# A two-block transformer kernel: modulation rows through GpSimd's queue, projection weights split after the squares' additions, a third gate tile ahead of the first latent product

## Chip, cores and metric

One core of one Trainium2 chip runs the whole program. The metric is device time in microseconds; of three timed executions the median counts.

## What is computed

256 tokens with 1024 channels pass through three layers: a retention layer, a latent-attention layer, each followed by a gated projection of a side input `p`, and a third layer with convolution, pooling and a feed-forward part, whose normalisations are modulated by a vector computed from `c_2`. Cut to what the change touches:

```python
# layers 0 and 1
h = rms_norm(x, pre_norm_g[i])
y = retention_branch(h, ...)  or  mla_branch(h, ...)     # both end in  (silu(gate) * o) @ w_out
x = x + rms_norm(y, post_norm_g[i])
x = x + (p[i] @ ple_w_proj[i]) * sigmoid(x @ ple_w_gate[i])
# inside mla_branch
c_q = rms_norm(z[..., :o1], q_norm_g); c_kv = rms_norm(z[..., o1:o2], kv_norm_g)
q = c_q @ w_uq                                           # the first latent product
# layer 2
mod = silu(c) @ w_ada + b_ada                            # 1024 x 6144, split in six vectors
h = layer_norm(x) * (1 + sc1) + sh1                      # and so on with g1, sh2, sc2, g2
```

All tensors are float32.

## The kernel before

Activations lie transposed, channels on partitions. Every large product is made exact enough by splitting: a weight tile `raw` of 128 x 1024 comes by DMA (512 KB), ScalarE rounds it to `wh` (L176, `A.copy`), VectorE subtracts to get the rest `wl` (L177, `V.tensor_sub`), and TensorE adds three products (`mm`, L232 to L234). One such load of eight 128 x 128 tiles feeds 24 matmuls. There are six buffers for `raw`, five each for `wh` and `wl`. `Seq` hands out the tiles of a list of entries in order and calls `load` whenever a new 1024-wide tile begins.

The program is written as one long stream. `tick` counts a nominal TensorE time, and `after(us, fn)` places side work (norm statistics, softmax steps) at a later point of that stream. But the order in which an engine gets its instructions is made by a planner at build time: whatever is ready in its plan and has a free buffer may go ahead of work that was written earlier and is not ready. Among ready instructions the earlier written one goes first. `tc.keep_in_program_order(i)` pins an instruction behind the last one that was written before it for the same engine. On the chip each engine then takes its instructions strictly in the planned order and waits at the head of its queue.

Three places matter.

- **Modulation rows.** `ada_steps` (L398 to L416) goes through 48 rows of 128 x 1024 of `w_ada`. `fetch` brings one row (512 KB) into one of two buffers `adach` (tag `ada1`); L408 multiplies it on VectorE with silu(c) and sums into a column of `mod`. The fetch of row n+2 stands behind the reduction of row n, goes through SP's queue and is pinned there, so it is issued at the point of the stream at which `ada()` is called. SP's queue also carries all weight fetches (L163). `mod_rate` sets how often `ada()` is called: every 10 us in the retention layer, every 1.8 us in the first part of `ret_out`, every 7.61 and 12.84 us in the latent layer. The last eight rows are called from `late_steps` near the end. They make `g2`, which goes to DRAM and back as a broadcast row (`g<-mod`, `half<-g`, L1366 and L1370) for the last normalisation.
- **Projection weights.** `out_proj` runs the layer's output product in two parts: the first twelve of sixteen blocks of channels for all eight outputs m, then the last four. In the second part `done` feeds finished pairs to `Sums`: ScalarE squares them (L322), VectorE adds the squares (L326, "the squares' additions"), and after m = 7 TensorE sums over channels with a matrix of ones (L336). The statistics (L374, L376, L362 to L368) follow, then `post` scales (L679), adds the residual (L680) and splits. `prepared()`, called in `post`, fetches and splits the two weight tiles of `p @ ple_w_proj` and multiplies them; that product fills TensorE while the statistics are made. These two loads are written behind all loads of the output product.
- **Gate tiles.** In the latent layer `mla_gate(g)` makes two of 16 gate blocks (two loads, 48 matmuls) and needs only the normalised input. `mla_proj(p)` is the first to need the latent vectors, which come out of `lora` (L772 to L780, split at L185 and L186). Two gate tiles are made ahead of `mla_proj(0)`, two more ahead of `mla_proj(1)`.

GpSimd's queue carries little: some memsets, the two fetches of `p` (L712), and at the end the broadcast rows and one addition.

Of the kernel before, what the change touches and what calls it, by code (L numbers as in the profile page):

```python
# [11 lines left out]
F32 = mybir.dt.float32  # L12
# [7 lines left out]
P = 128  # L20
# [62 lines left out]
def tile_kernel(ctx, tc, order, xT, pT, pos, vec, cst, cv, rows, wada, wts, outT):  # L83
    nc = tc.nc
    V, A, T = nc.vector, nc.scalar, nc.tensor
# [11 lines left out]
    def nm(s):  # L97
        uid[0] += 1
        return f"{s}_{uid[0]}"
# [4 lines left out]
    def bank2():  # L104
        return bank().rearrange("p (b t) -> p b t", b=2)

    class Blk:

        def __init__(self, nb, dt=F32):
            self.t = [hp_.tile([P, 4, S], dt, tag="half", name=nm("half")) for _ in range((nb + 3) // 4)]  # L110
# [21 lines left out]
    def t2(dt=F32):  # L132
        return tp.tile([P, 2, S], dt, tag="t2", name=nm("t2"), bufs=6)
# [6 lines left out]


    class Seq:
        def __init__(self, entries, width=P, parts=True, ready=()):
            self.e, self.w, self.i, self.parts, self.ready = entries, width, 0, parts, list(ready)

        def next(self):
            per = D // self.w
            s = self.i % per
            if s == 0:
                self.h, self.l = load(self.e[self.i:self.i + per], self.w, self.parts, self.ready.pop(0) if self.ready else None)  # L150
            self.i += 1
            sl = slice(s * self.w, (s + 1) * self.w)
            return self.h[:, sl], self.l[:, sl]

    def fetch(entries, width, parts=True, step=D, pinned=False):
        g = len(order)
        order.append((width, list(entries)))
        n = len(entries) * width
        tag, bufs = (("raw", 6), ("wh", 5), ("wl", 5))[0 if parts else [0, 1][g % len([0, 1])]]
        raw = wp.tile([P, D], F32, tag=tag, name=nm("raw"), bufs=bufs)  # L160
        for o in range(0, n, step):
            e = min(n, o + step)
            d = nc.sync.dma_start(out=raw[:, o:e], in_=wts[g, :, o:e])  # L163
            if pinned:
                tc.keep_in_program_order(d)
        return raw[:, :n]

    def load(entries, width, parts=True, raw=None):
        if raw is None:
            raw = fetch(entries, width, parts)  # L170
        if not parts:
            return raw, raw
        n = raw.shape[1]
        hi = wp.tile([P, D], F32R, tag="wh", name=nm("wh"), bufs=5)[:, :n]
        lo = wp.tile([P, D], F32R, tag="wl", name=nm("wl"), bufs=5)[:, :n]
        A.copy(hi, raw)  # L176
        V.tensor_sub(lo, raw, hi.bitcast(F32))  # L177
        return hi, lo

    def nouter(name, ms, kbs, c0=0):  # L180
        return [(name, kb * P, c0 + m * P) for m in ms for kb in kbs]

    def split(hi, lo, src, scale=None):
        if scale is None:
            A.copy(hi, src)  # L185
            V.tensor_sub(lo, src, hi.bitcast(F32))  # L186
        else:
            A.activation(hi, src, AF.Copy, scale=scale)
            V.scalar_tensor_tensor(lo, src, scale, hi.bitcast(F32), MUL, SUB)
# [11 lines left out]
    def after(us, fn):  # L201
        queue.append((clk[0] + us, fn))
        queue.sort(key=lambda e: e[0])
# [4 lines left out]
    def mod_rate(us):  # L208
        mods["rate"], mods["last"] = us, clk[0]
# [13 lines left out]
    def drain():  # L223
        busy[0] = True
        while queue:
            due, fn = queue.pop(0)
            clk[0] = max(clk[0], due)
            fn()
        busy[0] = False

    def mm(ps, l, r, first, last):
        T.matmul(ps, l[0], r[0], start=first, stop=False)  # L232
        T.matmul(ps, l[0], r[1], start=False, stop=False)  # L233
        T.matmul(ps, l[1], r[0], start=False, stop=last)  # L234
        tick(3 * r[0].shape[-1] / 2400.0)
# [5 lines left out]
    def rhs(pair, kb):  # L241
        return pair[0][kb], pair[1][kb]
# [35 lines left out]
    def col(name, i, n=1):  # L278
        o = VOFF[name] + i
        return vc[:, o:o + n]  # L280
# [117 lines left out]
    def ada_steps():  # L398
        def fetch(n):
            ch = sp.tile([P, D], F32, tag="ada1", name=nm("adach"), bufs=2)  # L400
            tc.keep_in_program_order(nc.sync.dma_start(out=ch, in_=wada[n * P:(n + 1) * P, :]))
            return ch

        have = [fetch(0), fetch(1)]
        yield
        for n in range(48):
            ch = have.pop(0)
            V.tensor_tensor_reduce(ch, ch, sc, 1.0, 0.0, MUL, ADD, mod[:, n:n + 1])  # L408
            if n + 2 < 48:
                have.append(fetch(n + 2))  # L410
            if n % 8 == 7:
                m = slice(n - 7, n + 1)
                V.tensor_add(mod[:, m], mod[:, m], col("b_ada_2", n - 7, 8))
            yield
# [11 lines left out]
    def ada():  # L426
        mods["n"] += 1
        next(ada_it, None)
# [181 lines left out]
    def out_proj(name, pairs, ka, rate, done, layer):  # L610
        ys = proj_banks()
        mod_rate(rate)
        seq = Seq(nouter(name, range(8), range(ka)) + nouter(name, range(8), range(ka, 16)))
        for m in range(8):
            for kb in range(ka):
                mm(ys.at(m), seq.next(), rhs(pairs, kb), ys.starts(m) and kb == 0, False)
        drain()
        mod_rate(None)
        prep = ple_proj(layer)
        for m in range(8):  # L620
            for kb in range(ka, 16):
                mm(ys.at(m), seq.next(), rhs(pairs, kb), False, kb == 15 and ys.ends(m))
            if ys.ends(m):
                done(m, ys)
        return ys, prep

    class proj_banks:
# [81 lines left out]
    def ple_proj(layer):  # L709
        php = [tp.tile([P, 2, S], F32R, tag="fa", name=nm("php"), bufs=3) for _ in range(2)]  # L710
        raw = t2()
        nc.gpsimd.dma_start(out=raw, in_=pT[:, 2 * layer:2 * layer + 2, :])  # L712
        split(php[0], php[1], raw)

        def prepared():
            seq = Seq(nouter(f"ple_proj{layer}", range(8), range(2)))
            tiles = [seq.next() for _ in range(16)]
            prj = Blk(DB)
            for i in range(4):
                ps = bank2()  # L720
                for b in range(2):
                    for kb in range(2):
                        mm(ps[:, b, :], tiles[(2 * i + b) * 2 + kb], (php[0][:, kb, :], php[1][:, kb, :]), kb == 0, kb == 1)
                A.copy(prj.pair(i), ps)
            return prj
        return prepared

    sums, done = proj_sums(False, lambda m, ys: ys.piece(m), "r")
    ys, prep = out_proj("ret_out", ret_g, 12, 1.8, done, 0)
    xt = post(xt, ys, sums, 0, prep)  # L730

# [54 lines left out]
    seq = Seq([e for kb in range(8) for e in (("mla_kr", kb * P, 0), ("mla_in", kb * P, 768), ("mla_in", kb * P, 896))])  # L786
# [9 lines left out]
    seq = Seq(nouter("mla_in", range(6), range(8)))  # L796
# [13 lines left out]
    def mla_gate(p):  # L810

        if p % 2 == 0:
            sgs[p // 2] = Blk(4)
        ps = bank2()
        for b in range(2):
            for kb in range(8):
                mm(ps[:, b, :], seq_g.next(), rhs(xp, kb), kb == 0, kb == 7)
        gr = t2()
        V.scalar_tensor_tensor(gr, ps, -0.5, bc2(r1["nr"]), MUL, MUL)
        A.activation(sgs[p // 2].pair(p % 2), gr, AF.Silu)  # L820
# [97 lines left out]
    mod_rate(7.61)  # L918
    ng = 0
    for p in range(8):  # L920
        while ng < [2, 4, 6, 8, 8, 8, 8, 8][p]:
            mla_gate(ng)
            ng += 1
        if p == 4:
            mod_rate(12.84)
        mla_proj(p)
        after(3.07, lambda p=p: mla_scores(p))

    sums, done = proj_sums(False, lambda m, ys: ys.piece(m), "m")
    ys, prep = out_proj("mla_out", mla_g, 12, 2.27, done, 1)  # L930
    xt = post(xt, ys, sums, 1, prep)

# [144 lines left out]
    def conv():  # L1077
        next(conv_it, None)
# [251 lines left out]
    seq = Seq([e for i in range(NA + 2, FB) for e in nouter("w_up", [i, FB + i], range(8))])  # L1330
# [6 lines left out]

    late = late_steps()
    after(1.12, lambda: every(2.6, 3 * NA + 8, lambda: next(late)))


# [3 lines left out]
    seq = Seq([("w_down", kb * P, 512 * n) for kb in kbs for n in range(2)], 512)  # L1345
# [137 lines left out]
```

## Time and profile before

| | |
|---|---|
| median of three executions | 851.39 us (851.32 to 853.29) |
| the profiled execution | 853.2 us, of which the span is 851.4 us |
| TensorE busy | 834.8 us, 98% |
| VectorE busy | 713.2 us, 84% |
| ScalarE busy | 550.6 us, 65% |
| GpSimd busy | 9.7 us, 1% |
| DMA | 167.5 MB, mean 197 GB/s; SP's queue holds 55.0% of the 16 engines' span, GpSimd's 0.9% |

Almost all of the span is TensorE's own work, so the table says little about where a change of order can matter. That is read from the waits of TensorE, and from what stands on the other engines just ahead of them.

### The profile page before, as it was taken

How to read it: one execution, taken by the hardware profiler on the slowest of the kernel's cores; microseconds unless marked ns; L12 is line 12 of the kernel's file. 1: busy time of each engine (PE TensorE's matmuls, PEld its weight loads, DVE VectorE, ACT ScalarE, POOL GpSimd, SP SyncE). 2: the span in 40 equal slices, each digit the busy share in tenths (PEclk: the TensorE clock that was granted, in tenths of full speed). 3: DMA queues.
4: the chain of work that ended last, by engine and by line, in shares of the span. 5: the costliest groups of instructions: out<-in, count | busy, mean ns of one | idle time of the engine just before them, and what ended most of it. 6: DMA issues, size and time to landing. Idle time of an engine off the chain costs nothing.

```text
span 851.4 us, 15952 instructions
## 1 busy us (share of the span) xinstructions
PE 834.8 (98%) x6218; PEld 798.2 (94%) x6218; DVE 713.2 (84%) x1287; ACT 550.6 (65%) x928; POOL 9.7 (1%) x28
## 2 busy tenths in 40 slices
PE   8999999999999999999999999999999999999995
PEld 6989899999999999999999998999999999999885
DVE  6999787898889978699874677899687888889996
ACT  6656555545676686787653757999756576666550
POOL 0000000000000000000000000000000000000001
PEclk9999999999999999999999999999999999999998
DMA  9866566678557647365355354245463365567722
GB/s 334 321 233 235 204 211 245 243 254 293 188 173 243 242 150 237 136 243 179 118 168 174 142 205 156 85 174 177 146 226 134 136 194 179 194 205 253 275 86 74
DMA packets 46634, 167.48 MB, mean 197 GB/s; under 512 B 5216, under 2 KB 5472, under 8 KB 46560
## 3 DMA queue, kind: packets, MB, share of 16 engines
q1 hardware_dynamic: 45936, 164.38, 55.0%
q0 software_dynamic: 624, 2.10, 0.9%
q8 instruction: 48, 0.79, 0.4%
q14 instruction: 26, 0.21, 0.1%
HBM read 165.41 MB, written 1.05 MB: 196 GB/s over the span
## 4 chain that ended last, share of the span: by engine, by line
PE 93%; DVE 4%; DMA 1%; ACT 1%; issue 1%; DVEq 0%; SPq 0%; ACTq 0%
PE ps L233 27%; PE ps L232 26%; PE ps L234 26%; PE ps L238 10%; PE ps L336 1%; PE ps L358 1%; DVE wl L177 1%; PE ps L898 1%; DMA adach<-in_wada 1%; DMA raw<-in_wts 1%; DVE half L679 0%; ACT wh L176 0%; DVE half L680 0%; PE ps L1146 0%; DVE t L1410 0%
## 5 line engine op out<-in xcount | busy, mean ns | idle before, releaser
L232 PE MATMUL ps<-half,wh 128*128 128x256 f32 x1504 | 424.8, 283 | 1.4 <-ACT half L185 1.4
L233 PE MATMUL ps<-half,wh 128*128 128x256 f32 x1504 | 423.6, 282 | 0.6 <-DVE half L186 0.5
L234 PE MATMUL ps<-half,wl 128*128 128x256 f32 x1504 | 422.1, 281 | 0.3 <-DVE wl L177 0.3
L176 ACT CAST wh<-raw 128x1024 fp32r<-128x1024 f32 x233 | 242.9, 1048 | 147.7 <-PE ps L233 94.3
L177 DVE TENSOR_TENSOR wl<-raw,wh 128x1024 fp32r<-128x1024 f32 x233 | 282.3, 1219 | 58.3 <-ACT wh L176 55.8
L233 PEld LDWEIGHTS ps<-half,wh 128*128 128x128 f32 x1504 | 283.3, 188 | 1.9 <-DVE half L186 0.9
L232 PEld LDWEIGHTS ps<-half,wh 128*128 128x128 f32 x1504 | 282.4, 188 | 2.6 <-ACT half L185 2.0
L234 PEld LDWEIGHTS ps<-half,wl 128*128 128x128 f32 x1504 | 283.9, 189 | 0.6 <-DVE wl L177 0.5
L238 PE MATMUL ps<-half,raw 128*128 128x256 f32 (+2 forms) x384 | 84.9, 380 | 0.0
L238 PEld LDWEIGHTS ps<-half,raw 128*128 128x128 f32 x384 | 72.5, 190 | 10.0
L232 PE MATMUL ps<-wh,half 128*128 128x512 f32 (+1 forms) x202 | 72.7, 361 | 0.0
L234 PE MATMUL ps<-wh,half 128*128 128x512 f32 (+1 forms) x202 | 71.0, 351 | 0.0
L233 PE MATMUL ps<-wl,half 128*128 128x512 f32 (+1 forms) x202 | 71.0, 351 | 0.0
L408 DVE CUSTOM_DVE_ANT_0 adach<-adach,siluc 128x1024 f32<-128x1024 f32 x48 | 58.3, 1218 | 11.5 <-DMA adach<-in_wada 11.5
L1063 ACT ACTIVATE t<-apad,vec 128x256 f32<-128x256 f32 x106 | 44.3, 500 | 0.5 <-DVE half L1064 0.5
L233 PEld LDWEIGHTS ps<-wl,half 128*128 128x128 f32 x202 | 38.1, 189 | 5.5 <-DVE wl L177 0.4
L232 PEld LDWEIGHTS ps<-wh,half 128*128 128x128 f32 x202 | 38.0, 188 | 5.5 <-ACT wh L176 0.2
L234 PEld LDWEIGHTS ps<-wh,half 128*128 128x128 f32 x202 | 38.0, 188 | 5.5
L1064 DVE TENSOR_TENSOR half<-half,t 128x512 f32<-128x512 f32 x53 | 36.4, 687 | 3.7 <-ACT t L1063 1.8
L185 ACT CAST half<-t 128x256 fp32r<-128x256 f32 (+1 forms) x47 | 20.3, 452 | 16.9 <-DVE t L1323 10.9
L186 DVE TENSOR_TENSOR half<-t,half 128x256 fp32r<-128x256 f32 (+1 forms) x47 | 21.7, 483 | 3.6 <-ACT half L185 2.7
L1318 ACT ACTIVATE t<-ps,vec 128x256 f32<-128x256 f32 x38 | 21.0, 558 | 2.0 <-PE ps L234 1.2
(277 smaller groups left out, 971.1 us busy)
## 6 DMA issues: line engine op xcount, KB each, us to landing
raw<-in_wts SPq DMA_DIRECT2D x257, 512.0 KB, 4.3
adach<-in_wada SPq DMA_DIRECT2D x48, 512.0 KB, 5.1
half<-in_xT SPq DMA_DIRECT2D x4, 256.0 KB, 6.9
half<-in_rows POOLq DMA_DIRECT2D x2, 512.0 KB, 5.2
out<-t SPq DMA_DIRECT2D x4, 256.0 KB, 2.0
cst<-in_cst SPq DMA_DIRECT2D x1, 928.0 KB, 10.1
raw<-in_wts SPq DMA_DIRECT2D x2, 256.0 KB, 5.1
siluc<-in_cv SPq DMA_DIRECT2D x1, 512.0 KB, 8.1
```

Of the source, the lines that this page charges most:

```text
L176: A.copy(hi, raw)
L177: V.tensor_sub(lo, raw, hi.bitcast(F32))
L185: A.copy(hi, src)
L186: V.tensor_sub(lo, src, hi.bitcast(F32))
L232: T.matmul(ps, l[0], r[0], start=first, stop=False)
L233: T.matmul(ps, l[0], r[1], start=False, stop=False)
L234: T.matmul(ps, l[1], r[0], start=False, stop=last)
L238: T.matmul(ps, w, r, start=first, stop=last)
L408: V.tensor_tensor_reduce(ch, ch, sc, 1.0, 0.0, MUL, ADD, mod[:, n:n + 1])
L1063: A.activation(t[:, b, :], apad[:, i0 + b, k:k + S], AF.Copy, scale=w[b])
L1064: V.tensor_add(acc.pair(i0 // 2), acc.pair(i0 // 2), t)
L1318: A.activation(t[:, b, :], ps[:, b, :], AF.Identity, bias=col("b_dw_f_2", m), scale=w[2])
```

## The change

The rows of `w_ada` are fetched through GpSimd's queue and no longer pinned. The two projection loads are written after m = 5 of the second part, ahead of the last load of the output product, and their subtractions are pinned behind what VectorE was last given, the second of the squares' additions. The first latent product stands behind three gate tiles; the second then stands behind one.

```diff
     class Seq:
-        def __init__(self, entries, width=P, parts=True, ready=()):
-            self.e, self.w, self.i, self.parts, self.ready = entries, width, 0, parts, list(ready)
+        def __init__(self, entries, width=P, parts=True, ready=(), pinned=False):
+            self.e, self.w, self.i, self.parts, self.ready, self.pinned = entries, width, 0, parts, list(ready), pinned
...
     def load(entries, width, parts=True, raw=None, pinned=False):
...
         A.copy(hi, raw)
-        V.tensor_sub(lo, raw, hi.bitcast(F32))
+        sub = V.tensor_sub(lo, raw, hi.bitcast(F32))
+        if pinned:
+            tc.keep_in_program_order(sub)
         return hi, lo
...
     def ada_steps():
         def fetch(n):
             ch = sp.tile([P, D], F32, tag="ada1", name=nm("adach"), bufs=2)
-            tc.keep_in_program_order(nc.sync.dma_start(out=ch, in_=wada[n * P:(n + 1) * P, :]))
+            nc.gpsimd.dma_start(out=ch, in_=wada[n * P:(n + 1) * P, :])
             return ch
...
             if ys.ends(m):
                 done(m, ys)
+            if m == 5:
+                prep.load()
         return ys, prep
...
+        tiles = []
+
+        def load():
+            seq = Seq(nouter(f"ple_proj{layer}", range(8), range(2)), pinned=True)
+            tiles.extend(seq.next() for _ in range(16))
+
         def prepared():
-            seq = Seq(nouter(f"ple_proj{layer}", range(8), range(2)))
-            tiles = [seq.next() for _ in range(16)]
             prj = Blk(DB)
...
+        prepared.load = load
         return prepared
...
     for p in range(8):
-        while ng < [2, 4, 6, 8, 8, 8, 8, 8][p]:
+        while ng < [3, 4, 6, 8, 8, 8, 8, 8][p]:
             mla_gate(ng)
```

## Rows read from the trace of the kernel before

**Rows 1.** The page: engines' busy time, share of the span, instructions.
```profile
PE 834.8 (98%) x6218; PEld 798.2 (94%) x6218; DVE 713.2 (84%) x1287; ACT 550.6 (65%) x928; POOL 9.7 (1%) x28
```

**Rows 2.** Waits of TensorE: line, releaser, us in total, times, longest.
```profile
PE ps L336 <- DVE t L326: 2.5, 1, 2.5
PE ps L232 <- ACT half L185: 1.4, 1, 1.4
...
PE ps L898 <- DVE sm L887: 0.7, 1, 0.7
```

**Rows 3.** Timeline of TensorE, 211 to 215.5 us: start, us, instruction, idle before.
```profile
211.05 0.28 PE L234 MATMUL ps<-half,wl 128*128 128x256 f32 x1
213.83 1.53 PE L336 MATMUL ps<-t,ones 128*128 128x256 f32 x6 [2.50 <-DVE t L326]
```

**Rows 4.** Timeline of VectorE, 204 to 219 us.
```profile
205.57 1.23 DVE L408 CUSTOM_DVE_ANT_0 adach<-adach,siluc 128x1024 f32<-128x1024 f32 x1 [1.59 <-DMA adach<-in_wada]
...
206.72 4.63 DVE L177 TENSOR_TENSOR wl<-raw,wh 128x1024 fp32r<-128x1024 f32 x4
...
213.00 0.68 DVE L326 TENSOR_TENSOR t<-t,t 128x512 f32<-128x512 f32 x1
...
216.06 0.42 DVE L374 TENSOR_SCALAR t<-ps 128x256 f32<-128x256 f32 x1 [1.25 <-PE ps L336]
```

**Rows 5.** Timeline of TensorE, 282 to 286 us.
```profile
282.86 0.28 PE L233 MATMUL ps<-half,wh 128*128 128x256 f32 x1
282.98 0.28 PE L234 MATMUL ps<-half,wl 128*128 128x256 f32 x1
284.62 0.62 PE L232 MATMUL ps<-half,wh 128*128 128x256 f32 x3 [1.37 <-ACT half L185]
```

**Rows 6.** Timeline of VectorE, 278 to 293 us.
```profile
284.80 1.42 DVE L186 TENSOR_TENSOR half<-t,half 128x256 fp32r<-128x256 f32 x4
...
288.65 0.75 DVE L186 TENSOR_TENSOR half<-t,half 128x256 fp32r<-128x256 f32 x2
```

**Rows 7.** The tile adach: its instructions, who waited, time to landing.
```profile
L401 SPq DMA_DIRECT2D adach<-in_wada x48: 327/425/1447, 12.6 to 797.0; - x48
...
DMA to landing us min/median/max: 3.5/5.1/9.0
```

**Rows 8.** The tile adach by stretch: us, VectorE's share of it, clock, DMA.
```profile
163.00:200.00 37.00, 13.23 (x12) 1.00 0.81 275
200.00:222.00 22.00, 2.58 (x3) 1.00 0.74 275
```

**Rows 9.** All engines by stretch: busy us of each, clock, DMA share, GB/s.
```profile
12.00:16.00 4.00, 3.99 (x17) 2.85 (x16) 4.00 (x9) 4.00 (x8) 0.00 (x0) 1.00 1.02 409
...
163.00:166.00 3.00, 3.00 (x28) 3.00 (x27) 3.00 (x7) 1.38 (x2) 0.00 (x0) 1.00 0.88 266
```

**Rows 10.** Chain that ended last, 0 to 24 us: start, us, what.
```profile
1.65 4.71 DMA raw<-in_wts
...
6.49 5.70 PE ps L238 x8
```

**Rows 11.** Timeline of GpSimd, 0 to 200 us.
```profile
1.50 0.52 POOL L755 MEMSET kr<- 64x512 f32 x1
```

**Rows 12.** DMA issues of 160 to 161 us, and of 434 to 435 us.
```profile
t<-in_pT POOLq DMA_DIRECT2D x1, 256.0 KB, 5.4
...
t<-in_pT POOLq DMA_DIRECT2D x1, 256.0 KB, 3.5
```

**Rows 13.** Timeline of VectorE, 326 to 337 us.
```profile
328.57 1.23 DVE L408 CUSTOM_DVE_ANT_0 adach<-adach,siluc 128x1024 f32<-128x1024 f32 x1 [2.06 <-DMA adach<-in_wada]
...
335.71 0.55 DVE L887 TENSOR_SCALAR sm<-sm,sm 128x128 f32<-128x128 f32 x2
```

**Rows 14.** Timeline of VectorE, 827 to 845 us.
```profile
834.11 0.69 DVE L1387 TENSOR_TENSOR t<-ps,half 128x512 f32<-128x512 f32 x1 [4.75 <-DMA half<-g]
...
841.54 1.38 DVE L1407 TENSOR_TENSOR t<-t,half 128x512 f32<-128x512 f32 x2
```

More of the change, by code (lines that the diff above doesn't have):

```diff
@@ L149, in next @@
             if s == 0:
-                self.h, self.l = load(self.e[self.i:self.i + per], self.w, self.parts, self.ready.pop(0) if self.ready else None)
+                self.h, self.l = load(self.e[self.i:self.i + per], self.w, self.parts, self.ready.pop(0) if self.ready else None, self.pinned)
             self.i += 1
@@ L166, in fetch, with load @@
         return raw[:, :n]
-    def load(entries, width, parts=True, raw=None):
+    def load(entries, width, parts=True, raw=None, pinned=False):
         if raw is None:
```

## The prediction

> **What bounds the kernel now.** I began with the page: TensorE is busy 834.8 us, 98% of the span [rows 1]. No change of order can shorten that work, so the change is worth what it takes from TensorE's waits or adds to them. The second view is therefore the list of TensorE's waits [rows 2]. Past the start and the end of the program only three are over half a microsecond: 2.5 us for the squares' addition at L326, 1.4 us for a split of a latent vector at L185, 0.7 us for a softmax step at L887. Together that is 4.6 us, 0.54% of 851.39. A measurement of this kernel can tell about 0.3%, 2.55 us, from no change: faster means below 848.84, slower above 853.94.
>
> The third view is the timelines at these places. TensorE ends the second part of `ret_out` at 211.3 and starts the sums at 213.83, 2.50 us idle [rows 3]. VectorE shows why: at 205.57 a reduction L408 starts after waiting 1.59 us for its row, then four subtractions L177 run until 211.35, and the second addition L326 comes only at 213.00 [rows 4]. By the order of the fetches, the second and third of these four are the projection's two tiles. At the second place TensorE ends gate tile 1 at 283.3 and finds the first latent vector at 284.62 [rows 5]; the last latent split ends at 289.4 [rows 6].
>
> **The change, part by part.** The sum goes against the profiled execution's span, 851.4; it took 853.2, 1.8 us around the span. The median of the runs shown, 851.39, is 1.8 us under that execution; I carry the differences over to the median.
>
> *Third gate tile.* It moves 48 matmuls between 283.3 and the first latent product. Matmuls start 0.12 us apart there (282.86 to 282.98 [rows 5]), so the tile takes 5.8 us and TensorE arrives at 289.1, when four of the six latent vectors are long split [rows 6]; the last two need 0.3 us more and are used last. The 1.37 us [rows 5] go: **-1.4**, between -1.5 and 0. The tile's two loads come out of the same list earlier and hold two of five weight buffers while the latent vectors are made, which cover them. What is late next is the stretch up to `mla_proj(1)`, which loses 5.8 us of gates ahead of its softmax; its own gate tile and 7.6 us of planned distance cover that.
>
> *Projection subtractions.* Two subtractions of 1.16 us (4.63 over four [rows 4]) leave the stretch ahead of L326: 2.3 us of the 2.50 [rows 3]. They then stand behind the second addition. Queued behind them on VectorE are the statistics, L374; those wait for the sums anyway, and VectorE had 1.25 us idle there [rows 4], so about half of the 2.3 us comes back as delay of L374 if gate subtractions stand there too. I take **-1.3**, between -2.5 and 0. The two weight fetches pass the last output load in SP's queue and hold two `raw` and two `wh`/`wl` buffers longer; all that follows in that queue are gate weights, needed after the projection's own products. In the latent layer the wait does not show, and I cost the same edit there at nothing: VectorE has the matmuls of m = 6 and 7 to hide it, else it costs 2.3 us at most.
>
> *Rows through GpSimd.* Forty-eight issues of 0.425 us [rows 7] leave SP's queue, and no TensorE wait names a weight fetch past the start, so this alone gives nothing. What decides is the lost pin. The planner takes whatever is ready: GpSimd clears `kr` at 1.50 us [rows 11], though `kr` belongs to the latent layer. Two row buffers are free from the start, so I expect the first two fetches at about 1.5 us instead of 12.6 [rows 7]. There the transfers are the bound: TensorE's first product waits for a weight tile that takes 4.71 us to land [rows 10]. Two rows are 1.05 MB; at 409 GB/s [rows 9] that is 2.6 us of all DMA engines ahead of what TensorE waits for. If the two queues together move only 266 GB/s, as in the stretch in which GpSimd's fetch of `p` ran beside SP's [rows 9], it is 3.9 us; if the fetches are held or slip into gaps, 0. TensorE runs without a break behind that wait [rows 10], so a delay is never made up. I take **+2.5**, the nearest full-rate row.
>
> The Trainium skill speaks to this in "DMA: Bandwidth & Descriptors", section "Issuing engines are not separate DMA queues": transfers from any issuing engine run on the same 16 DMA engines and interleave, and a second issuer saves only issue time. The 266 GB/s agree with it in that the second queue brought no rate. By this rule no transfer of the change gets faster, and the start keeps its price.
>
> From then on a row is fetched as soon as its buffer is free, and reductions fill every idle moment of VectorE in the plan. By now 12 of them stand in 163 to 200 and 3 in 200 to 222 [rows 8], none in the statistics. Each takes 1.15 us (205.57 to 206.72 [rows 4]). With data always ready one may stand in the idle 1.25 us ahead of L374 [rows 4]; one that starts near the end of that moment delays the statistics by nearly its 1.15. I take **+0.8**, between 0 and 3.5 (three of them in full). In the softmax stretch the row that VectorE waited 2.06 us for [rows 13], just ahead of L887, would have landed long before: **-0.7** [rows 2], between -0.7 and +0.7. At the end, `g2` is ready early and the 4.75 us wait for its broadcast goes [rows 14]; VectorE then does the first half's products, 1.38 us at L1407 [rows 14], ahead of the last chunks. TensorE's own last products hold most of that back, so **-0.4**, between -0.5 and 0. The memsets and the fetch of `p` on GpSimd now queue behind row fetches that wait for VectorE, a few us; `p` has over 30 us until its product.
>
> Sum: 2.5 + 0.8 - 0.7 - 0.4 - 1.3 - 1.4 = -0.5. **Forecast 850.9 us**, no change that can be told.
>
> **Rivals.** *The start is not hit.* If the first two fetches do not float to the front, or their packets fit between SP's, the 2.5 us go: -0.5 - 2.5 = -3.0, **848.4**, faster. For it: the late landing of `silu(c)`, which the first reductions also need, gives a fetch at 1.5 us no use, and a planner may order by need. Against: it filled GpSimd at 1.50 with a memset far ahead of its use [rows 11].
>
> *Reductions in the way of the statistics.* The place is VectorE from 206 to 222. If three reductions stand there and the projection's gain is lost to them, it is 2.5 + 3.45 - 0.7 - 0.4 - 1.4 = +3.5, **854.9**, slower; with two it is +2.3 and not told from no change, so it decides from the third. For it: today the rows are limited by landing there (1.59 us of wait [rows 4]), the buffers are refilled at once, and nothing ends the row work at 206 any more. Also for it: GpSimd's fetch of 256 KB landed after 5.4 us where VectorE was busy throughout, after 3.5 us elsewhere [rows 12]. Against: higher-standing work goes first when both are ready.
>
> The Trainium skill, "SBUF — State Buffer", section "Who interferes with whom", would have a transfer issued from GpSimd starve while VectorE works in a two-port mode, since GpSimd cannot write the descriptors then. By it rows land later and the backlog reaches further into the statistics, this rival's time. The two landings lean that way, with one sample each.
>
> *The change does not do what it says:* the planner already had the projection's subtractions or the row fetches about where they now are, and only the gate tile counts, 851.39 - 1.4 = **850.0**.
>
> **How the numbers follow.** Forecast 0.49, start not hit 0.30, reductions in the way 0.17, only the gate tile 0.04. So faster 0.30, same 0.49 + 0.04 = 0.53, slower 0.17. The range reaches from 847.2 (the start not hit and 1.2 us more of the projection's gain) to 854.8 (just under the slow rival's middle); about 0.06 lie below and 0.12 above. The forecast's own range is 848.9 to 853.4.
>
> **What would show it.** In the trace of the changed kernel: the time of GpSimd's first two `adach` issues, and whether TensorE's first L238 starts near 6.5 or near 9 us. The wait of L336 for L326 and the count of L408 between 206 and 222. The wait of L232 for L185 near 284 gone. The wait of L1387 for `half<-g` gone. The forecast is wrong if L238 starts on time, or if any wait of TensorE over 2 us appears that rows 2 do not have.

## The result and the profile after

The changed kernel takes **899.66 us** (median of 4 runs, 897.33 to 903.42) against 852.34 us for the kernel before on the same chip (851.32 to 854.68): ratio **1.0547**, 95% interval 1.052 to 1.0574. The forecast was 850.9 us in a range of 847.2 to 854.8; the slowest rival had 854.9, so none of the cases came near. The profiled execution has a span of 895.6 us, 44.2 us over the span of before. Line numbers are slightly higher now: row fetch L403, reduction L410, squares' addition L328, ones-sums L338, group sums L360, products L234 to L236, splits L187 and L188; L176 and L177 kept theirs.

The page of the changed kernel: TensorE's busy time, the granted clock in 40 slices, and the issues of the rows.

```profile
PE 845.6 (94%) x6218; PEld 807.9 (90%) x6218; DVE 715.7 (80%) x1287; ACT 547.6 (61%) x927; POOL 35.3 (4%) x76
...
PEclk9999999999689999999999989999999999999999
...
adach<-in_wada POOLq DMA_DIRECT2D x48, 512.0 KB, 4.9
```

Against [rows 1] the work of VectorE is the same (713.2 and 715.7 us); TensorE has idle time that it hadn't, and three slices with a lower clock. The list of TensorE's waits names the places (line, releaser, us in total, times, longest):

```profile
PE ps L338 <- DVE t L328: 17.2, 2, 15.3
PE ps L234 <- ACT half L187: 9.5, 2, 5.2
PE ps L234 <- ACT t L187: 5.2, 3, 2.7
PE ps L360 <- DVE t L299: 4.1, 1, 4.1
PE ps L240 <- DMA raw<-in_wts: 3.4, 1, 3.4
```

In [rows 2] the first of these was 2.5 us in all, and the splits of the heads and the group sums did not appear. To see where the time went I take the start of the n-th matmul in both timelines and subtract. At matmul 60 (20.1 us before: the start), 1440 (202.0: the four heads are done), 1620 (227.3: past the sums and the projection of the first output), 2640 (351.9: latent attention), 3900 (502.0: past the sums of the second output) and 6180 (837.6: the end), TensorE is late by the following, in us. Each row comes from one profiled execution, and the runs in it are described in the experiments below.

| kernel | 60 | 1440 | 1620 | 2640 | 3900 | 6180 |
|---|---|---|---|---|---|---|
| changed kernel | 1.7 | 17.7 | 39.8 | 36.5 | 44.4 | 44.3 |
| gate tile alone | 1.2 | 1.1 | 0.8 | -2.0 | -1.9 | -1.9 |
| rows alone | 2.9 | 18.3 | 26.3 | 24.0 | 24.0 | 24.0 |
| projection alone | -0.5 | -0.6 | 7.0 | 8.3 | 18.2 | 18.2 |
| rows in SP's queue, no pin | -0.1 | 7.7 | 12.8 | 11.4 | 11.4 | 11.4 |
| rows, first two pinned | -0.2 | 13.8 | 21.8 | 19.6 | 19.5 | 19.5 |
| rows, reductions in place | 2.8 | 4.0 | 12.0 | 10.7 | 21.6 | 21.6 |
| projection behind the last load | -0.5 | -0.6 | -0.3 | -0.1 | 1.5 | 1.4 |

Differences of about 1 us between two traces say little: at matmul 60 the kernels whose start is unchanged already differ by -0.5 to 1.2. So 16 us went in the heads, where the prediction had no term at all, 22 us around the first sums, 8 us around the second; some 3 us came back between them.

**The first sums.** VectorE's timeline of the changed kernel (start, us, instruction, idle before):

```profile
224.91 1.22 DVE L410 CUSTOM_DVE_ANT_0 adach<-adach,siluc 128x1024 f32<-128x1024 f32 x1 [1.51 <-DMA adach<-in_wada]
...
229.36 1.22 DVE L410 CUSTOM_DVE_ANT_0 adach<-adach,siluc 128x1024 f32<-128x1024 f32 x1 [3.22 <-DMA adach<-in_wada]
...
234.62 1.23 DVE L410 CUSTOM_DVE_ANT_0 adach<-adach,siluc 128x1024 f32<-128x1024 f32 x1 [4.03 <-DMA adach<-in_wada]
...
235.77 0.69 DVE L328 TENSOR_TENSOR t<-t,t 128x512 f32<-128x512 f32 x1
239.99 1.23 DVE L410 CUSTOM_DVE_ANT_0 adach<-adach,siluc 128x1024 f32<-128x1024 f32 x1 [3.53 <-DMA adach<-in_wada]
...
241.14 0.69 DVE L328 TENSOR_TENSOR t<-t,t 128x512 f32<-128x512 f32 x1
241.74 4.62 DVE L177 TENSOR_TENSOR wl<-raw,wh 128x1024 fp32r<-128x1024 f32 x4
```

From 222 to 241 VectorE does next to nothing but wait for one row after the other: it is idle for 12.3 us (1.51 + 3.22 + 4.03 + 3.53) ahead of four reductions, and the two additions that TensorE needs stand behind the third and the fourth. ScalarE is not what they wait for: it had ended the last of their squares at 227.62. The next row is fetched only when a reduction has freed its buffer; in [rows 4] the one reduction near this place had waited 1.59 us. Then come four subtractions: the pinned two of the projection first, the last output load's third. So the products of m = 6 and 7, which had stopped at 226.6 after two matmuls each, had to wait as well. TensorE's timeline around the wait, where [rows 3] had 2.50 (the third product of each block, L236, is missing ahead of it):

```profile
226.11 0.28 PE L235 MATMUL ps<-half,wh 128*128 128x256 f32 x1
226.23 0.28 PE L234 MATMUL ps<-half,wh 128*128 128x256 f32 x1
226.35 0.28 PE L235 MATMUL ps<-half,wh 128*128 128x256 f32 x1
241.97 0.77 PE L338 MATMUL ps<-t,ones 128*128 128x256 f32 x1 [15.35 <-DVE t L328]
```

**The second sums** show the projection's part by itself, for no reduction is near (VectorE, 498 to 518 us):

```profile
498.96 1.23 DVE L177 TENSOR_TENSOR wl<-raw,wh 128x1024 fp32r<-128x1024 f32 x1 [1.64 <-ACT wh L176]
510.79 0.69 DVE L328 TENSOR_TENSOR t<-t,t 128x512 f32<-128x512 f32 x1 [10.60 <-ACT t L324]
513.62 0.69 DVE L328 TENSOR_TENSOR t<-t,t 128x512 f32<-128x512 f32 x1 [2.13 <-ACT t L324]
514.23 4.62 DVE L177 TENSOR_TENSOR wl<-raw,wh 128x1024 fp32r<-128x1024 f32 x4
```

VectorE is idle for 10.60 us and does not use it for the last output load's subtraction: that one is the third of the four at 514.23.

**The heads.** One of several like places (VectorE, 97 to 108 us); L297 and L299 feed the group sums L360, which waited 4.1 us:

```profile
103.76 1.23 DVE L410 CUSTOM_DVE_ANT_0 adach<-adach,siluc 128x1024 f32<-128x1024 f32 x1 [4.46 <-DMA adach<-in_wada]
...
104.91 0.69 DVE L297 TENSOR_TENSOR t<-t,t 128x512 f32<-128x512 f32 x1
...
105.91 0.41 DVE L299 TENSOR_TENSOR t<-t 128x256 f32<-128x256 f32 x1
```

The tile `adach` in the changed kernel: how long VectorE sat idle ahead of its reductions (us, times), and the time from issue to landing.

```profile
  DMA adach<-in_wada: 32.4, 20
...
DMA to landing us min/median/max: 3.6/4.9/8.3
```

Before, this idle time was 11.5 us in 11 waits, and the landing was as long [rows 7].

### The profile page after: what moved, and what is told of

It is laid out like the page before. It is cut to its first block, busy times and chain, and to the rows that moved or that the text cites. A ratio compares the mean times of both kernels' runs of the same rounds, so it can differ in the third digit from the quotient of the medians.

```text
span 895.6 us, 15985 instructions
## 1 busy us (share of the span) xinstructions
PE 845.6 (94%) x6218; PEld 807.9 (90%) x6218; DVE 715.7 (80%) x1287; ACT 547.6 (61%) x927; POOL 35.3 (4%) x76
## 4 chain that ended last, share of the span: by engine, by line
PE 69%; issue 17%; DVE 6%; DMA 4%; POOL 2%; ACT 2%; SPq 0%; DVEq 0%; POOLq 0%; ACTq 0%
PE ps L234 19%; PE ps L235 19%; PE ps L236 19%; PE ps L240 9%; DMA adach<-in_wada 3%; POOL adach L403 2%; DVE wl L177 2%; PE ps L338 1%; DMA half<-in_xT 1%; DVE adach L410 1%; ACT wh L176 1%; PE ps L908 1%; PE ps L360 1%; DVE half L191 0%; PE ps L1156 0%
## 5 line engine op out<-in xcount | busy, mean ns | idle before, releaser
L234 PE MATMUL ps<-half,wh 128*128 128x256 f32 x1504 | 428.1, 286 | 9.5 <-ACT half L187 9.5
L236 PE MATMUL ps<-half,wl 128*128 128x256 f32 x1504 | 424.3, 282 | 0.0
L177 DVE TENSOR_TENSOR wl<-raw,wh 128x1024 fp32r<-128x1024 f32 x233 | 282.4, 1220 | 60.1 <-ACT wh L176 57.6
L176 ACT CAST wh<-raw 128x1024 fp32r<-128x1024 f32 x233 | 241.8, 1048 | 126.0 <-PE ps L235 88.1
L234 PEld LDWEIGHTS ps<-half,wh 128*128 128x128 f32 x1504 | 285.9, 191 | 10.8 <-ACT half L187 10.3
L235 PEld LDWEIGHTS ps<-half,wh 128*128 128x128 f32 x1504 | 286.4, 190 | 1.1 <-DVE half L191 0.3
L236 PEld LDWEIGHTS ps<-half,wl 128*128 128x128 f32 x1504 | 286.5, 191 | 0.0
L410 DVE CUSTOM_DVE_ANT_0 adach<-adach,siluc 128x1024 f32<-128x1024 f32 x48 | 58.4, 1221 | 32.5 <-DMA adach<-in_wada 32.4
L234 PE MATMUL ps<-wh,half 128*128 128x512 f32 (+1 forms) x202 | 72.9, 362 | 0.0
L236 PE MATMUL ps<-wh,half 128*128 128x512 f32 (+1 forms) x202 | 71.2, 352 | 0.0
L1073 ACT ACTIVATE t<-apad,vec 128x256 f32<-128x256 f32 x106 | 44.2, 497 | 0.5 <-DVE half L1074 0.5
L236 PEld LDWEIGHTS ps<-wh,half 128*128 128x128 f32 x202 | 38.1, 189 | 5.6
L234 PEld LDWEIGHTS ps<-wh,half 128*128 128x128 f32 x202 | 38.0, 188 | 5.5 <-ACT wh L176 0.4
L403 POOL DMA_DIRECT2D adach<-in_wada x48 | 25.7, 535 | 222.7 <-DVE mod L410 214.0
L187 ACT CAST half<-t 128x256 fp32r<-128x256 f32 (+1 forms) x47 | 20.4, 452 | 16.8 <-DVE t L1333 12.1
L187 ACT CAST half<-half 128x512 fp32r<-128x512 f32 (+1 forms) x24 | 11.9, 512 | 26.1 <-DVE half L600 13.6
```

Source lines behind the costliest of these rows:

```text
L177: sub = V.tensor_sub(lo, raw, hi.bitcast(F32))
L403: nc.gpsimd.dma_start(out=ch, in_=wada[n * P:(n + 1) * P, :])
L1073: A.activation(t[:, b, :], apad[:, i0 + b, k:k + S], AF.Copy, scale=w[b])
```

## The experiments

My theory at this point: rows and projection each cost by themselves. The rows cost since VectorE works through its instructions in an order fixed beforehand, and without the pin the reductions stand where their row was supposed to have landed, with needed work behind them. The projection costs since the last output load's subtraction is handed out behind the pinned ones. The rivals: GpSimd's queue itself (slower or later transfers), and one of the two parts being harmless without the other.

**The gate tile alone.**

```diff
-        while ng < [2, 4, 6, 8, 8, 8, 8, 8][p]:
+        while ng < [3, 4, 6, 8, 8, 8, 8, 8][p]:
```

> Third gate tile alone. My theory: it is the one part that gains; the trace of the changed kernel has no idle at the first latent vector and is 1.7 to 3.4 us less late from there to the softmax stretch, so 849 to 851 us, ratio 0.996 to 0.999, and no other wait of TensorE over 1 us that the kernel before has not. Rival (the tile only moves the wait to the softmax of the next latent stretch): 851 to 852, with a wait of 1 us or more near 330.

Measured 851.31 us (10 runs), ratio 0.996, interval 0.9943 to 0.9976. TensorE's wait of 1.4 us for L185 is gone; it gains 2.8 us between matmul 1620 and 2640 (0.8 to -2.0), of which 2.0 are waits of TensorE that went (2.4 to 0.4 us in that stretch); where the rest comes from is not traced. One wait over 1 us is new (1.6 us for `wh`, L176); it lies in the first 20 us, which the edit doesn't touch. This version is faster than both kernels, by 0.4% against the one before.

**The rows alone**, through GpSimd without a pin:

```diff
-            tc.keep_in_program_order(nc.sync.dma_start(out=ch, in_=wada[n * P:(n + 1) * P, :]))
+            nc.gpsimd.dma_start(out=ch, in_=wada[n * P:(n + 1) * P, :])
```

> Rows through GpSimd's queue without a pin, nothing else. My theory: this is the larger cause. Reductions stand in VectorE's order where the row is supposed to have landed, and the critical work behind them waits; up to the third head TensorE loses what it lost in the changed kernel there, 1.7 at the start and about 2, 6, 6 and 2 us near 47, 106, 131 and 174, together 17 to 18; then the reductions of rows 38 to 43 stand among the squares' additions and cost some 10 to 16 more: 868 to 886 us. Rival (the pinned projection subtractions are what makes the 15 us wait of the sums, and reductions only fill the gap that they leave): 868 to 871, the sums' wait under 3 us.

Measured 877.47 us, ratio 1.0266 (1.0227 to 1.0304). TensorE's longest waits and VectorE's timeline, 224 to 239 us, of this run:

```profile
PE ps L336 <- DVE t L326: 8.5, 1, 8.5
PE ps L358 <- DVE t L297: 4.9, 2, 4.1
```

```profile
227.91 1.23 DVE L408 CUSTOM_DVE_ANT_0 adach<-adach,siluc 128x1024 f32<-128x1024 f32 x1 [2.20 <-DMA adach<-in_wada]
...
229.06 2.36 DVE L177 TENSOR_TENSOR wl<-raw,wh 128x1024 fp32r<-128x1024 f32 x2
233.28 1.23 DVE L408 CUSTOM_DVE_ANT_0 adach<-adach,siluc 128x1024 f32<-128x1024 f32 x1 [1.85 <-DMA adach<-in_wada]
...
235.56 0.69 DVE L326 TENSOR_TENSOR t<-t,t 128x512 f32<-128x512 f32 x1
...
237.30 0.69 DVE L326 TENSOR_TENSOR t<-t,t 128x512 f32<-128x512 f32 x1
238.57 1.23 DVE L408 CUSTOM_DVE_ANT_0 adach<-adach,siluc 128x1024 f32<-128x1024 f32 x1 [0.58 <-DMA adach<-in_wada]
```

The loss of the heads is all here (18.3 us late at matmul 1440), and so is a wait of 8.5 us for the additions: the rival, under 3 us, falls. The softmax wait at L898 of [rows 2] is gone, and so, without the gate tile, is the wait for the latent vector's split at L185: 26.3 to 24.0. The gate tile has nothing left to gain beside the rows.

**Pin or queue.** The rows left in SP's queue and only the pin taken away:

```diff
-            tc.keep_in_program_order(nc.sync.dma_start(out=ch, in_=wada[n * P:(n + 1) * P, :]))
+            nc.sync.dma_start(out=ch, in_=wada[n * P:(n + 1) * P, :])
```

> Rows left in SP's queue, only the pin of their fetch taken away. If the lost pin is the cause of what the rows cost (ratio 1.027 with GpSimd), the reductions drift here as well and the time is 865 to 885 us, ratio 1.015 or more, with reductions between the squares' additions of the first output projection. If GpSimd's queue is the cause, the time is that of before within 3 us.

Measured 866.38 us, ratio 1.0147 (1.013 to 1.0165), at the low end of the theory's bound. A reduction does stand between the squares' additions (it starts at 221.33, the additions at 220.38 and 223.62), and the additions were waited for 5.4 us:

```profile
PE ps L336 <- DVE t L326: 5.4, 1, 5.4
```

The lost pin alone makes over half of the rows' 2.7%. The rest comes with GpSimd, and the next run says how much of that is the start.

**The first two rows pinned in SP's queue, the others through GpSimd without a pin:**

```diff
+            if n < 2:
+                tc.keep_in_program_order(nc.sync.dma_start(out=ch, in_=wada[n * P:(n + 1) * P, :]))
+            else:
+                nc.gpsimd.dma_start(out=ch, in_=wada[n * P:(n + 1) * P, :])
```

> Rows through GpSimd without a pin, but the first two rows pinned in SP's queue as before. This prices the start alone. By the prediction's term it takes 2.5 us off the 877 us of the rows alone (874 to 875), and TensorE's first product on a weight tile starts near 6.5 us instead of 8.9. Rival: the delay at the start is not lasting (the later waits take it up), and the time stays at 877 within 1 us.

Measured 870.61 us, ratio 1.0186 (1.0152 to 1.022). TensorE is no longer late at matmul 60 (-0.2 against 2.9): the start is real, and lasting. The time is below the forecast of 874 to 875: the whole gain is larger than the start, 4.5 us at the last matmul, because the heads lose less too (14.0 us against 15.4). Against the unpinned rows in SP's queue 0.4% is left for GpSimd; the two intervals overlap. In the two traces it is more, 19.5 against 11.4 us at the last matmul, most of it in the heads; but the executions of this run lie between 867.28 and 873.00 us, and the profiled one is the slowest. So its size stays open.

**The fetch held to its place.** To undo the loss of the pin but keep GpSimd, each fetch was made to wait for the weight tile fetched last:

```diff
+            nc.gpsimd.tensor_copy(ch[:, 0:1], lastraw[0][:, 0:1])
+            nc.gpsimd.dma_start(out=ch, in_=wada[n * P:(n + 1) * P, :])
```

> Rows through GpSimd, but each fetch held to its written place: ahead of it GpSimd copies one column out of the weight tile that was fetched last in the written order, so it can't start before that tile has landed. If the lost pin is the cause, the reductions stand about where they stood before (none from 207 to 255 us) and the time is 849 to 855 us. If the queue is the cause (slower landings, an issue that waits on VectorE), 865 us or more.

Measured 913.53 us, ratio 1.0702 (1.0672 to 1.0732): my theory's 849 to 855 was far off. The reductions did stand about where they stood before (27 ahead of the sums, none between 229 and 285 us), but VectorE stood idle ahead of them for 70.6 us (tile `adach`), and weight fetches in SP's queue waited for the copy, which holds the weight tile until the row's buffer is free (waits of SP's queue):

```profile
  DMA adach<-in_wada: 70.6, 26
```

```profile
SPq L166 <- POOL adach L404: 53.1, 14, 7.0
```

So the place on the time axis is not the point; a fetch that begins late for the place of its reduction is. As a test of GpSimd's queue the run is void, for the hold itself delays weights. To tell these two apart, the same hold with the reductions pinned as well:

```diff
+            red = V.tensor_tensor_reduce(ch, ch, sc, 1.0, 0.0, MUL, ADD, mod[:, n:n + 1])
+            if n < 40:
+                tc.keep_in_program_order(red)
```

> The held fetch (a column copied out of the last weight tile ahead of each row's fetch on GpSimd) together with reductions of rows 0 to 39 pinned to their written place. It asks why the held fetch alone cost 7%. If VectorE stood at reductions that the planner had put at a landing that came later on the chip (70.6 us in 26 waits), written places some 20 us behind the fetch take most of that away: idle at reductions under 20 us and 865 to 880 us, near the two runs with pinned reductions. If it was GpSimd's held queue or the copy that holds weight tiles longer, the time stays over 895 us.

Measured 897.44 us, ratio 1.0507 (1.0471 to 1.0543). The idle time fell to 31.4 us, not under 20, and 16 us came back, so part of the 7% was VectorE at rows that had not landed; but over 895 us is also what the hold was to give. Both are in it, and their shares stay open.

**Reductions in their written place, fetch free on GpSimd.** The same pin on the reductions of rows 0 to 39, without the hold:

> Rows through GpSimd with no pin on the fetch, but the reductions of rows 0 to 39 pinned on VectorE to their written place. Rows are then fetched as soon as a buffer is free and are reduced some 20 us of written order later. If what costs is VectorE standing at a reduction whose row has not landed (24.0 us of it in the rows alone, 70.6 us where the fetch was held, 11.5 before), that idle time falls under 3 us, and of the rows' 23 us only the start (2 to 7 us) stays: 853 to 860 us. If GpSimd's queue itself costs, 865 us or more.

Measured 875.21 us, ratio 1.0251 (1.0212 to 1.0291): the total missed 853 to 860 and lies where GpSimd's queue was to be the cause. The idle time at reductions missed as well; it did not fall under 3 us but is what the rows alone had, 24.0 (tile `adach`):

```profile
  DMA adach<-in_wada: 24.4, 15
```

Where it lies speaks for the place of the reductions all the same. In the heads VectorE still stands idle for 8.2 us ahead of five reductions, and TensorE does not wait for it: idle time at a row costs something only where work stands behind it that TensorE needs soon. The waits of TensorE from 20 to 190 us are an empty list; it goes from 2.8 us late at matmul 60 to 4.0 at 1440, where the rows alone went from 2.9 to 18.3. Same queue, same free fetches, and only the reductions' place differs. In the heads GpSimd's queue therefore costs no more than about 1 us, and the place of the reductions 14. The loss moved to the sums:

```profile
PE ps L336 <- DVE t L326: 12.1, 2, 8.3
PE ps L238 <- DMA raw<-in_wts: 4.3, 1, 4.3
```

The written order has a reduction every 1.8 us of planned time around the first output projection; two buffers and a landing of some 4 us don't allow that, and the last 6 rows, unpinned, were drawn into 466 to 494 us, ahead of the second sums (3.8 us of the 12.1); 10.9 us of VectorE's idle time lie ahead of these six.

**The same pin with the rows in SP's queue as before:**

> Rows as before in SP's queue with their pin, and the reductions of rows 0 to 39 pinned to their written place. If the 11.5 us that VectorE stands at reductions before matter to TensorE at all, this gains up to the 2.5 us wait at L326 (848.5 to 850.5 us); if they are slack, it is the time of before within 1.5 us; if a reduction in its written place comes in the way of a chain that it now passes, 855 us or more.

Measured 864.69 us, ratio 1.0121 (1.0078 to 1.0164), the third outcome. The wait at L336 grew from 2.5 to 7.1 us, and a softmax step is waited for 3.4 us. In the kernel before the reductions float ahead of their written place as far as the pinned fetches let them, 27 of them by 206 us, and so the sums stay almost free. The order before was a balance between two wrong ones: later (this run) and earlier (rows alone). Set beside the run before it, this one is 10.8 us less late at the last matmul (10.8 against 21.6): 3.1 are the start, 1.3 the heads, 1.4 the first sums, and 4.7 arise around the second sums, where this run has no rows: it reduces its last six only from 776 us on.

```profile
PE ps L336 <- DVE t L326: 7.1, 1, 7.1
PE ps L900 <- DVE sm L889: 3.4, 1, 3.4
```

**The projection alone**, the diff of the change without its rows and gate tile:

```diff
+            if m == 5:
+                prep.load()
```

> Projection weights handed out at m = 5 with the pinned subtractions, rows as before. My theory: the pinned subtractions stand behind the second squares' addition, and the subtraction of the last output load, written after them, stands behind them; TensorE stops after the first product of m = 6 and 7 and again ahead of the gate. In the changed kernel this cost 7.9 us in the latent layer, where no reduction is near; the same in the first layer gives 851.4 + 15 to 16 = 866 to 868 us, with two waits for the additions of about 2 us and two for the gate's halves of about 4 us. Rival (the loss in the first layer is all due to reductions): 858 to 860 us, the waits in the latent layer alone.

Measured 871.42 us, ratio 1.0194 (1.0162 to 1.0226): over the forecast, since TensorE lost 9.9 us in the latent layer where the changed kernel had lost 7.9. The first layer loses 7.6 with the reductions as before, so the rival falls. Waits and VectorE's timeline of this run:

```profile
PE ps L234 <- ACT half L187: 10.0, 3, 4.2
PE ps L338 <- DVE t L328: 3.9, 2, 2.0
```

```profile
209.54 0.69 DVE L328 TENSOR_TENSOR t<-t,t 128x512 f32<-128x512 f32 x1 [1.47 <-ACT t L324]
210.15 5.76 DVE L177 TENSOR_TENSOR wl<-raw,wh 128x1024 fp32r<-128x1024 f32 x5
```

**Without the pin**, the same place:

```diff
-            seq = Seq(nouter(f"ple_proj{layer}", range(8), range(2)), pinned=True)
+            seq = Seq(nouter(f"ple_proj{layer}", range(8), range(2)), pinned=False)
```

> As the projection alone, but its subtractions without a pin. If the pin is the cause, the planner puts the two subtractions into VectorE's idle time, the last output load's follows at once, and the loss goes: 850 to 854 us. If the place where the weights are handed out is the cause (five buffers in written order, two of them held longer), most of the 15 us stay: 860 us or more.

Measured 854.81 us, ratio 1.0007 (0.9992 to 1.0021): the pin is what costs. The subtractions went back ahead of the additions; the wait at the first sums became 2.0 us for the last output load's `wl` and 0.7 for the additions, together what it was.

**Behind the last output load.** Handed out one product later, when m = 6 has its weights, and held behind the second addition (by an explicit dependence, since the pin would now hold them behind the last output load's subtraction only):

```diff
-            if m == 5:
-                prep.load()
+                if m == 6 and kb == ka:
+                    prep.load()
...
-            tc.keep_in_program_order(sub)
+            tc.add_manual_dep(sub.ins, lastadd[0].ins.name, mybir.DependencyInfo(
+                mybir.DependencyClass.NoSync, mybir.DependencyReason.DATA), reason="behind the addition")
```

> Projection weights alone, handed out after the last output load instead of ahead of it, and their subtractions held behind the second squares' addition. If the order in which the five buffers are handed out is what made the last output load wait, its subtraction now comes ahead of the additions, the 2.5 us wait at L326 of before shrinks to under 1.2 and nothing takes its place: 848.5 to 850.5 us, ratio 0.997 to 0.999. If the hold behind the addition is bad by itself, the gate's halves still wait about 4 us in each layer: 860 us or more.

Measured 858.58 us, ratio 1.005 (1.0033 to 1.0066). It answers both halves. The order of handing out, together with the pin, is what made the disaster: with the last output load's subtraction ahead, the additions wait 0.5 us instead of 2.5, and the wait ahead of the gate is 1.9 us instead of 4.2. Waits of TensorE, 200 to 240 us (L341 and L331 are this run's lines of the ones-sums and the additions):

```profile
PE ps L235 <- ACT half L188: 1.9, 1, 1.9
PE ps L341 <- DVE t L331: 0.5, 1, 0.5
```

But the gain that I had forecast is not there either. The two subtractions push the two of the gate behind them into the statistics, and TensorE waits 1.9 us for the gate's halves in each layer, in the latent one for no gain at all. My 848.5 to 850.5 was wrong.

**The parts together.** The whole change with that order of handing out:

> The whole change, but the projection weights handed out behind the last output load. If the parts add up, this takes away the projection's 1.9% less the 0.5% that this order costs by itself: ratio 1.040. If the matmuls of m = 6 and 7 are the cover of the late squares' additions, which the change took away, the parts don't add up, the 15.3 us wait shrinks to that of the rows alone (8.5), and the ratio is that of rows, gate tile and this order together: 1.026 to 1.030.

Measured 887.37 us, ratio 1.0385 (1.0324 to 1.0445): the parts' sum, not the lost cover. From matmul 1440 to 1620 it loses 14.7 us, the changed kernel 22.1, the rows alone 8.0. Putting the matmuls of m = 6 and 7 back ahead of the wait removed what the projection costs alone (7.6) and no more. Two more runs, the change without its gate tile and the change with its rows as before:

> The change without its gate tile: rows and projection together. The three parts alone multiply to 1.042 (0.996 x 1.0266 x 1.0194), the change measures 1.0547. If the rest is between rows and projection, this is at 1.055 or more; if it is between the gate tile and one of them (the tile has nothing left to gain where the other parts shift the wait), this is 1.0466 to 1.050.

> The change with its rows as before: gate tile and projection together. If the parts add up here, 0.996 x 1.0194 gives 1.015 (867 us); if the gate tile loses its gain beside the projection, 1.019. And the rows' share inside the change is then the change's 1.0547 over this ratio: 1.035 to 1.039, against 1.0266 alone.

Measured 1.0531 (1.0501 to 1.0561) and 1.0135 (1.0115 to 1.0155). The first lies between the two outcomes named for it, the second is a little under both. Rows and projection together cost some 0.65% over their product (1.0266 x 1.0194 = 1.0465), just clear of what the three intervals leave open. In the trace TensorE is late by 20.0 us between matmul 1440 and 1620, against 8.0 + 7.6 for the two alone. The gate tile keeps its gain beside the projection (1.0194 to 1.0135) and loses it beside the rows (1.0531 to 1.0547, intervals that overlap). So the rest has two likely sources: some 0.65% between rows and projection, and the gate tile's 0.4%. In the trace the first looks like this: with the rows alone, two projection subtractions run while VectorE's row is under way (229.06), hidden; pinned behind the additions they can't. And with the rows alone the second addition, at 237.30, comes ahead of the next reduction; in the changed kernel one more row, waited for 3.53 us, stands ahead of it. Both are read, not tested.

## Why the prediction was wrong

- **The drift of the reductions: +0.8, at most 3.5. The step that failed.** Measured in the rows alone: 21.1 us (24.0 less 2.9 of the start). The step priced a misplaced reduction at its own 1.15 us on VectorE, "three of them in full". What a misplaced reduction costs is the rest of its row's landing, for all work behind it on VectorE that TensorE needs soon: up to 4.5 us each. The landing of 3.5 to 9.0 us and a wait of 1.59 stood in [rows 7] and [rows 4]. And the prediction took "with data always ready" for granted: with two buffers and a landing of 4.9 us a denser run of reductions is never ready. The Trainium skill says in "PSUM — Partial Sum Buffer", section "Engine vs sequencer instructions", that VectorE's queue is strictly first in, first out. The trace agrees: both additions stood behind reductions that had nothing to do for 3.5 and 4.0 us.
- **The place.** The prediction looked for drift where TensorE waited before, in 206 to 222. Two thirds of the rows' loss arose in the heads (15.4 of 24.0 us), where [rows 2] has no wait. The slow rival had the mechanism's place and sign for the sums and gave 854.9.
- **The projection: -1.3, and nothing in the latent layer. Failed too.** The step named the statistics as what is queued behind the pinned subtractions. The last output load's subtraction is, as it takes the same five buffers and is written later; m = 6 and 7, named as the cover in the latent layer, were the work that had to wait. Measured +7.6 and +9.9 us. The gain itself falls with the run behind the last load: 2 us less at L336, 1.9 more at the gate.
- **The start: +2.5. Right.** GpSimd's first row fetches were issued at 1.27 and 2.30 (forecast 1.5), and TensorE's first product on a weight tile began at 8.32 instead of 6.49 [rows 10]: 1.8 us, 2.4 in the rows alone. That start varies by itself, so one pair proves little; but all eleven traces that don't let rows ahead of the weights have it between 5.80 and 6.78, and all five that do, between 8.05 and 9.08.
- **The third gate tile: -1.4. Right in kind, short in size alone (2.8 us), no gain shown beside the rows.** The wait for L185 is gone in the changed kernel, as it is without the tile once the rows are reduced early.
- **Softmax -0.7: the wait is gone, but not shown to be for the reason given.** It is gone as well in the projection alone, with and without its pin, where the rows are fetched as before; so whether the term came true for its reason or by luck is open. **The end -0.4: nothing** came (44.4 to 44.3 us late), though VectorE's wait for `half<-g` is gone, as forecast.
- **Transfers through GpSimd's queue are not slower.** A row issued there landed as fast as before (median 4.9 against 5.1 us, longest 8.3 against 9.0). The Trainium skill's rule in "SBUF — State Buffer", section "Who interferes with whom", that such a transfer starves beside VectorE's two-port work, does not show in these landings; it is not tested by them either, for no run shows in which mode VectorE worked. The Trainium skill's other rule that the prediction used, in "DMA: Bandwidth & Descriptors", section "Issuing engines are not separate DMA queues", is that a second issuer saves only issue time; the trace agrees, with landings alike through both queues. What the queue costs otherwise stays open: with the pin off, rows on GpSimd are 12.6 us later at the last matmul than rows in SP's queue (24.0 against 11.4), 3.0 of it at the start and 7.6 in the heads. No run shows whether that is all due to the places which the planner then gives to the reductions.

## What to carry to other kernels

A pin on a transfer may be the only thing that holds its consumers in place: before taking it away, ask where the planner will put every one of them, and price each at the wait for its data, wherever work stands behind it that another engine needs soon, and not at its own duration. When an instruction is pinned, list what is handed out after it from the same buffers, for that waits as well. And look for drift where the engine in question is full, not only where TensorE waits now.

## What the runs showed of the hardware

The granted clock made the long waits dearer than their length. All engines by stretch in the changed kernel (busy us of each engine, then the clock, DMA share, GB/s):

```profile
131.20:133.00 1.80, 1.67 (x7) 1.57 (x8) 1.80 (x4) 1.42 (x3) 0.00 (x0) 0.50 0.72 241
...
226.60:242.00 15.40, 0.05 (x2) 0.06 (x1) 5.08 (x9) 1.89 (x5) 1.55 (x3) 0.60 0.23 81
242.00:246.00 4.00, 4.00 (x15) 3.64 (x16) 4.00 (x4) 0.16 (x1) 0.05 (x1) 0.50 0.71 215
246.00:250.00 4.00, 4.00 (x32) 4.00 (x32) 2.64 (x4) 1.34 (x3) 0.53 (x1) 0.89 0.95 335
...
259.70:264.00 4.30, 4.30 (x19) 4.23 (x20) 4.30 (x10) 1.30 (x3) 0.00 (x0) 0.51 0.33 127
264.00:268.00 4.00, 4.00 (x36) 4.00 (x35) 4.00 (x8) 2.35 (x5) 0.53 (x1) 1.00 0.28 79
```

After the idle 15.35 us the clock was at its lower level of 1.2 GHz (0.50) for 4 us of work and more. The same followed the 5.2 us ahead of the gate: 19 matmuls in 4.3 us at 0.51, and then 36 in 4.0 us at 1.00. Smaller waits differ: after 2.68 us at 131 the clock fell to 0.50, after the 2.50 us before [rows 3] it stayed at 1.00; what made the difference is not shown. I had not counted any of this. TensorE's busy time, for the same 6218 matmuls, rose by 10.8 us (834.8 to 845.6); as an estimate from these two numbers, about a quarter of the 44.2 us lost is the lower clock and the rest is waiting. The clock also goes with the spread of nearly equal executions: the projection behind the last load has one with a clock of 0.997 and a span of 853.3 us, the others have 0.993 to 0.994 and 855.1 to 857.6.
